# A hybrid decoder step: inputs in a second, turned layout, channel-major normalisation, token-major memory values, two outputs that leave turned

## The chip, the cores and the metric

The kernel runs on one core of a Trainium2 chip. Five engines issue their instructions in order, each from a list of its own: PE (matrix products; a transpose is a product with an identity matrix), ACT (activations, casts and copies), DVE (vector operations), POOL (GpSimd) and SP, which here only issues DMAs; ACT also issues some. An engine goes on to its next instruction only when everything that this instruction waits for is there. The metric is the device time of one execution in microseconds, as the median of several runs. The host's preparation of the arrays is not part of it.

## The reference, cut to what matters

Prompt and sample tokens (1024 and 8, 1032 together, 1024 channels each) go through one layer:

```
h    = x * rsqrt(mean(x*x) + EPS) * norm_g            # per token, over channels
proj = h @ w_in                                       # 7688 columns: q, k, v, beta, alpha, gates, ...
ya, S, buf = delta_branch(q, k, v, ...)               # causal conv, SiLU, gated delta rule
yb, vn = chunk_mlp_branch(u, v, gate, ...)            # LayerNorm, 128x128 position mixing
yc   = memory_branch(q, gate, mem_k, mem_v)           # attention into 256 memory tokens
y    = x + (sum of gates * (branch @ w_br)) @ w_out   # then a final RMSNorm

def memory_kv(mem, mem_norm_g, w_mem_kv):
    kv = rmsnorm(mem, mem_norm_g) @ w_mem_kv
    k, v = jnp.split(kv, [C_WIDTH], axis=-1)          # both are outputs: (256, 4, 128)

def causal_conv(buf, x, w):                           # 1536 channels, 4 taps
    xp = jnp.concatenate([buf.astype(x.dtype), x], axis=1)
    ...
    return jax.nn.silu(y), xp[:, -(CONV_WIDTH - 1):]  # the last three rows are an output too
```

## The kernel before, in words

**Products.** Every large product is made in three passes over a rounded high part and the rest: hi·hi, hi·lo and lo·hi, each over the KT = 8 blocks of 128 channels (`mm3`), so 24 matmuls per group. The normalised input stands channel-major, as hTh and hTl: partition = channel in its block, then block, then token. Tokens are taken in three groups of 344; one projected tile of 128 output channels (k0, v0, q0 for head 0, and so on) is 72 matmuls. `h_group` makes one group into a PSUM buffer pj, of which there are two; an `evac` function, mostly a copy on ACT, empties it. tp (two buffers) and dl (four) are the other PSUM buffers.

**Weights.** `order` lists every job's weight slice of 128 columns. `w_load` starts its load three jobs ahead, from ACT's queue; `w_split` casts it one job ahead (whi on ACT, L250) and subtracts (wlo, on DVE unless another engine is named, L253).

**Order of the work.** The order on each engine is the order in which the code emits it. The jobs run one after another as the plans say: `plan_a` (per head k, v, q, the gate ag, tiles of branch B and merge gates), `plan_c` (gates, eight kv jobs of the memory, then cq and cg) and `plan_m` (branch projections). Everything else is a generator in `Streams`: after every sixth matmul `tick` moves each generator to its next yield, so its instructions come to lie between matmuls. `run.until(condition)` moves the generators on without emitting matmuls between them.

**The start.** Rows of x are loaded token-major on SP in tiles of 128 tokens. `n_square` (L366) squares and sums on ACT, `n_newton` makes the reciprocal root in eleven small steps on DVE, `n_scale` scales rows by root and norm_g on DVE, and `n_turn` transposes eight blocks on PE, casts them to hTh on ACT (L393) and subtracts to hTl on DVE (L394). Tiles 0 and 1 are done ahead; `norm_gen` (L436) does the rest between the matmuls of k0 and v0, which run in four parts of 256, 256, 256 and 264 tokens, each as soon as its rows are ready. `const_gen` turns the small vectors and the old convolution state on PE. Then comes q0 as an ordinary job, then the product with wab, the 8 columns of beta and alpha (L583).

**The delta stream.** After that `delta_all` is added: for each head `delta_gen` (L733) waits for its k, v and q and walks through the chunks; the last chunk's products stand in L909 to L918, the result r is scaled in L931 (r by ro) and, two ticks later, turned by eight transposes, from which ag is multiplied and stored as ya. `conv_gen` (L482) runs for each k, v and q tile: it turns the last 11 columns of the raw projection (xraw, two buffers, copied in L531), copies the rows and stores them to the two state outputs, then convolves. When plan_a is through, `run.until(("delta", 3) in done)` finishes the stream.

**The memory.** `mem_norm` (L291) normalises 256 rows like the start. A kv job makes a tile of 128 columns of keys or values, channel-major (kvT, copied in L1132); `kv_gen` splits keys as they are, turns every tile on PE, stores the rows, and splits values from the rows. `b_gen` (L1034) first turns the four w_spatial blocks on PE.

The jobs of the plans and the rule of the streams, as they stand:

```python
    plan_a = [
        [("k", 0), ("v", 0), ("q", 0), ("ag", 0), ("bv", 0), ("bv", 1), ("bv", 2)],
        [("k", 1), ("v", 1), ("q", 1), ("ag", 1), ("bv", 3), ("bg", 0), ("bu", 0)] + gates(1),
        [("k", 2), ("v", 2), ("q", 2), ("ag", 2), ("bg", 1), ("bu", 1), ("bg", 2), ("bu", 2)],
        [("k", 3), ("v", 3), ("q", 3), ("ag", 3), ("bg", 3), ("bu", 3)] + gates(7),
    ]
    ...
            PE.matmul(out, lhsT=w, rhs=r, start=(i == 0), stop=(i == len(ops) - 1))
            if ticks and i % 6 == 5:
                tick()
```

Of the kernel before, what the change touches and what calls it, by code (L numbers as in the profile page):

```python
# [21 lines left out]
P = 128  # L22
# [19 lines left out]
    ("x_sample", (NB, D)),  # L42
    ("cache_mem_k", (NB, MEM, H, P)),
# [4 lines left out]
    ("norm_g", (D,)),  # L48
    ("w_in", (D, 7688)),
    ("conv_w", (4, 1536)),  # L50
    ("a_log", (H,)),
    ("dt_bias", (H,)),
    ("a_norm_g", (P,)),
    ("ln_v_g", (512,)),
    ("ln_v_b", (512,)),
    ("w_spatial", (H, P, P)),
    ("b_spatial", (H, P)),
    ("mem_norm_g", (D,)),
# [4 lines left out]
    ("b_gate", (3, D)),  # L63
# [55 lines left out]
def tile_mixer_step(ctx: ExitStack, tc: tile.TileContext, a):  # L119
# [64 lines left out]
    c_bg, c_cw, c_an = 16, 40, 88  # L184
# [8 lines left out]
    # ---- weights: loaded three jobs ahead, split one job ahead  # L193
# [7 lines left out]
    def gates(n):  # L201
# [4 lines left out]
        [("k", 0), ("v", 0), ("q", 0), ("ag", 0), ("bv", 0), ("bv", 1), ("bv", 2)],  # L206
# [83 lines left out]
    # ---- RMSNorm of the inputs, transposed and split  # L290
    def mem_norm(np_, srcs, g_bc, dst_h, dst_l):  # L291
        ss = np_.tile([P, 2], F32, tag="nss", name="mss")
        r = np_.tile([P, 2], F32, tag="nrs", name="mrs")
        xs = []
        for i, src in enumerate(srcs):
            x = np_.tile([P, D], F32, tag="x", name="x")
            SP.dma_start(out=x, in_=src)
            xs.append(x)
        yield 6
        for i, x in enumerate(xs):  # L300
            xn = np_.tile([P, D], F32, tag="xn", name="xn", bufs=2)
            S.activation(out=xn, in_=x, func=AF.Square, accum_out=ss[:, i:i + 1])
# [3 lines left out]
        for i, x in enumerate(xs):  # L306
            xn = np_.tile([P, D], F32, tag="xn", name="xn", bufs=2)
            V.scalar_tensor_tensor(
                out=xn, in0=x, scalar=r[:, i:i + 1], in1=g_bc, op0=ALU.mult, op1=ALU.mult
            )  # L310
            yield 2
            cs = slice(i * P, (i + 1) * P)
            for b in range(2):
                t = tp().rearrange("p (k n) -> p k n", k=4)
                for k in range(4):
                    kk = b * 4 + k
                    transpose(t[:, k], xn[:, kk * P:(kk + 1) * P])
                split(dst_h[:, b * 4:b * 4 + 4, cs], dst_l[:, b * 4:b * 4 + 4, cs], t)
                yield 1
            done.add(("mem", i))  # L320
# [1189 lines left out]
```

## Time and profile before

| | before |
|---|---|
| median of 3 runs | 1152.01 us |
| lowest and highest run | 1151.9 and 1152.84 us |
| span of the profiled execution | 1148.6 us |
| PE busy | 1119.7 us (97%), 7609 instructions |
| DVE busy | 609.7 us (53%) |
| ACT busy | 411.9 us (36%) |
| POOL busy | 214.1 us (19%) |
| PE's waits for scaled rows at the start | 12.7 us, 2 times, the longest 10.4 us |
| mean granted PE clock | 0.995 |

The profiled execution's own time is its span, from its first to its last instruction; the runs are timed from outside and lie 3.4 us above it in the median. A busy time is the sum over an engine's instructions; the columns "PEld" in the profile are PE's weight loads, which lie beside its products. In a row of groups stand the code line, the engine, the operation, the tile written and the tile read, shapes, the count, and then busy time and mean duration, then the idle time before them and what ended it. Line numbers are those of the kernel before; where the text says that a line is of the changed kernel, it is that one's own.

### The profile page before, as it was taken

To read this page: it belongs to the slowest core of one execution; us is meant where nothing else is said; L and a number is where in the kernel's file an instruction comes from. 1 tells how busy PE (TensorE), PEld (TensorE's weight loads), DVE (VectorE), ACT (ScalarE), POOL (GpSimd) and SP (SyncE) were. 2 spreads that over 40 slices of the span, in tenths; PEclk is the share of its full clock that TensorE was granted. 3 is DMA by queue.
4 is the path that set the end of the run, shared out by engine and by line. 5 is a ranking of instruction groups with operands and counts; after the bars stand their busy time and mean duration, and the time that the engine had idled before them with its cause. 6 is when DMAs were issued, how large, how long until landed. Compare 5 with 4: busy or idle time off the path is not lost.

```text
span 1148.6 us, 19257 instructions
## 1 busy us (share of the span) xinstructions
PE 1119.7 (97%) x7609; PEld 1074.8 (94%) x7609; DVE 609.7 (53%) x1512; ACT 411.9 (36%) x891; POOL 214.1 (19%) x392
## 2 busy tenths in 40 slices
PE   5999999999999999999999999999999999999997
PEld 4989999999999999999999999989999999998884
DVE  6754654655465546513277432655545246786554
ACT  5434233333331333333344333545445321232232
POOL 1060715070507050600034000101101000000000
PEclk9999999999999999999999999999999999999999
DMA  8104420341143114422654556543432465662221
GB/s 250 39 20 97 132 63 23 117 129 46 40 125 104 45 41 126 124 79 77 200 138 137 166 170 186 159 118 93 146 114 74 145 195 176 212 213 100 83 93 57
DMA packets 153772, 133.53 MB, mean 116 GB/s; under 512 B 20941, under 2 KB 134922, under 8 KB 153674
## 3 DMA queue, kind: packets, MB, share of 16 engines
q1 hardware_dynamic: 72242, 89.82, 24.5%
q10 hardware_dynamic: 81440, 42.49, 13.7%
q8 instruction: 60, 0.98, 0.3%
q14 instruction: 30, 0.25, 0.1%
HBM read 100.74 MB, written 31.64 MB: 115 GB/s over the span
## 4 chain that ended last, share of the span: by engine, by line
PE 90%; DVE 4%; DMA 2%; ACT 2%; issue 1%; SPq 1%; ACTq 0%; DVEq 0%
PE pj L275 56%; PE dl L275 20%; PE tp L191 2%; PE dl L191 2%; PE dl L784 1%; DMA raw<-w_in 1%; DMA stg<-ya 1%; PE dl L894 1%; PE tp L1094 1%; PE dl L918 1%; PE dl L909 1%; PE dl L902 1%; PE dl L904 1%; PE dl L917 1%; DVE wlo L253 1%
## 5 line engine op out<-in xcount | busy, mean ns | idle before, releaser
L275 PE MATMUL pj<-hTh,whi 128*128 128x344 f32 (+1 forms) x1456 | 280.7, 327 | 3.1 <-DVE ql L155 1.1
L275 PE MATMUL pj<-hTh,wlo 128*128 128x344 f32 (+1 forms) x1456 | 277.5, 325 | 0.0
L275 PE MATMUL pj<-hTl,whi 128*128 128x344 f32 (+1 forms) x1456 | 272.3, 322 | 0.0
L275 PEld LDWEIGHTS pj<-hTh,whi 128*128 128x128 f32 x1456 | 232.4, 190 | 5.9 <-ACT hTh L393 1.5
L275 PEld LDWEIGHTS pj<-hTh,wlo 128*128 128x128 f32 x1456 | 235.1, 189 | 1.4 <-issue 0.8
L275 PEld LDWEIGHTS pj<-hTl,whi 128*128 128x128 f32 x1456 | 234.3, 188 | 1.1 <-DVE hTl L394 0.2
L253 DVE TENSOR_TENSOR wlo<-raw,whi 128x1024 fp32r<-128x1024 f32 (+1 forms) x91 | 102.5, 1126 | 51.7 <-ACT whi L250 44.2
L250 ACT CAST whi<-raw 128x1024 fp32r<-128x1024 f32 (+1 forms) x92 | 86.2, 937 | 81.5 <-PE dl L275 64.8
L957 ACT COPY stg<-pj 128x344 f32<-128x344 f32 x72 | 32.1, 446 | 108.0 <-PE pj L275 107.6
L838 POOL TENSOR_TENSOR itmp<-X,Lt 128x60 f32<-128x60 f32 (+24 forms) x124 | 43.7, 352 | 125.7 <-DMA Lt<-ld 116.5
L1184 POOL TENSOR_TENSOR kvt<-kvt,qb 128x1024 f32<-128x1024 f32 x8 | 19.2, 2419 | 210.7 <-DMA qb<-qd 130.9
L275 PE MATMUL dl<-yh,whi 128*128 128x344 f32 x288 | 57.3, 321 | 0.0
L275 PE MATMUL dl<-yh,wlo 128*128 128x344 f32 x288 | 57.3, 321 | 0.0
L275 PE MATMUL dl<-yl,whi 128*128 128x344 f32 x288 | 57.1, 320 | 0.0
L275 PEld LDWEIGHTS dl<-yh,whi 128*128 128x128 f32 x288 | 47.8, 188 | 0.0
L275 PEld LDWEIGHTS dl<-yh,wlo 128*128 128x128 f32 x288 | 47.7, 188 | 0.0
L275 PEld LDWEIGHTS dl<-yl,whi 128*128 128x128 f32 x288 | 47.6, 188 | 0.0
L844 POOL TENSOR_TENSOR X<-X,itmp 128x60 f32<-128x60 f32 (+24 forms) x124 | 43.7, 353 | 9.7
L531 ACT COPY xraw<-pj 128x344 f32<-128x344 f32 (+2 forms) x38 | 16.3, 430 | 66.4 <-PE pj L275 63.1
L906 DVE COPY y<-dl 128x128 f32<-128x128 f32 x32 | 9.3, 291 | 55.3 <-PE dl L904 34.4
L1367 DVE TENSOR_TENSOR stg<-dl,stg 128x344 f32<-128x344 f32 x48 | 24.7, 515 | 18.1 <-PE dl L275 18.1
L503 POOL TENSOR_TENSOR kq<-kq,cvt 128x512 f32<-128x512 f32 x24 | 32.6, 1358 | 1.9
(378 smaller groups left out, 1591.9 us busy)
## 6 DMA issues: line engine op xcount, KB each, us to landing
raw<-w_in ACTq DMA_DIRECT2D x57, 512.0 KB
gate<-stg SPq DMA_DIRECT2D x23, 516.0 KB
stg<-gate SPq DMA_DIRECT2D x23, 516.0 KB
x<-x_prompt SPq DMA_DIRECT2D x8, 512.0 KB
raw<-w_mem_kv ACTq DMA_DIRECT2D x8, 512.0 KB
kvt<-cache_mem_k SPq DMA_DIRECT2D x16, 256.0 KB
kvt<-cache_mem_v SPq DMA_DIRECT2D x16, 256.0 KB
wor<-w_out SPq DMA_DIRECT2D x8, 512.0 KB
```

The costliest lines, as they stand in the source:

```text
L191: PE.transpose(out, in_, ident[:p, :p])
L250: S.copy(out=hi, in_=raws[i])
L253: eng.tensor_tensor(out=lo, in0=raws[i], in1=f32(hi), op=ALU.subtract)
L275: PE.matmul(out, lhsT=w, rhs=r, start=(i == 0), stop=(i == len(ops) - 1))
L503: G.tensor_tensor(out=d[:, cs], in0=d[:, cs], in1=o, op=ALU.add)
L531: S.copy(out=raw[:, 3 + sl.start:3 + sl.stop], in_=o)
L784: PE.matmul(t, lhsT=kq[:, 0, sl], rhs=kq[:, :, sl], start=True, stop=True)
L838: G.tensor_tensor(out=tm, in0=X[:, 0:m, j:j + 1].to_broadcast([P, m, n]), in1=Lt[:, j:j + 1, j + 1:32].to_broadcast([P, m, n]), op=ALU.mult,)
L844: G.tensor_tensor(out=X[:, 0:m, j + 1:32], in0=X[:, 0:m, j + 1:32], in1=tm, op=ALU.subtract)
L957: project("gate", i, lambda n, sl, o: S.copy(out=t[:, sl], in_=o))
L1184: G.tensor_tensor(out=kts[hb], in0=kts[hb], in1=qb[:, hb * 4:hb * 4 + 4].unsqueeze(2).to_broadcast([P, 4, 2, P]), op=ALU.mult,)
L1367: V.tensor_tensor(out=sg[:, sl], in0=o, in1=sg[:, sl], op=ALU.mult)
```

## The change

The host now also passes the inputs in turned layouts and turns two outputs back: `x_t` and `mem_t` are x and the memory channel-major, (128, 8, tokens); `cols` holds norm_g, mem_norm_g, b_gate, conv_w and a_norm_g as 89 columns; `conv_old` and `w_spatial_t` are the convolution state and the spatial matrices turned. `x_prompt`, `x_sample` and `mem_prompt` are still read token-major as well, for the sums of squares and the residual. The new convolution state leaves channel-major (`conv_new`, 11 columns per channel) and the memory keys leave channel-major (`mk_t`). On the device:

- 1/rms is spread over the partitions by a product of a matrix of ones with a diagonal matrix (`spread`), and x_t is scaled in place, block by block, by the channel's norm_g and that row (`scale`), then split. Transposes of x, of the memory, of the vectors, of the convolution state and of w_spatial are gone.
- The start runs over four parts of tokens; the tiles are k0, v0 and bv0, which moves ahead of q0 in plan_a.
- A convolution tile stores its 11 columns straight from xraw.
- Memory values are made token-major: four kv jobs each take two blocks of 128 input channels and all 512 value columns, adding up in two dl buffers; `v_gen` copies, splits and stores them. Memory keys are stored and split as they are made.

The core of the diff:

```diff
-        [("k", 0), ("v", 0), ("q", 0), ("ag", 0), ("bv", 0), ("bv", 1), ("bv", 2)],
+        [("k", 0), ("v", 0), ("bv", 0), ("q", 0), ("ag", 0), ("bv", 1), ("bv", 2)],
...
+    def spread(np_, rs, tiles):
+        t = dl()
+        at = 0
+        for i, n in tiles:
+            dg = np_.tile([P, P], F32, tag="dg", name="dg", bufs=2)[:n, :n]
+            V.tensor_scalar(out=dg, in0=ident[:n, :n], scalar1=rs[:n, i:i + 1], scalar2=None, op0=ALU.mult)
+            PE.matmul(t[:, at:at + n], lhsT=ones[:n], rhs=dg, start=True, stop=True)
+            at += n
+        return t[:, :at]
+
+    def scale(x, r, col, k):
+        V.scalar_tensor_tensor(
+            out=x[:, k], in0=x[:, k], scalar=colv[:, col + k:col + k + 1], in1=r, op0=ALU.mult, op1=ALU.mult
+        )
...
+    x_load(0, 1)
+    xt_load(0)
+    SP.dma_start(out=colv, in_=a["cols"])
     w_load(0, SP)
     w_load(1, SP)
+    x_load(2, 3)
+    xt_load(1)
     w_load(2, SP)
+    x_load(4)
...
+    def n_split(n, b, eng=V):
+        ks = slice(b * 4, b * 4 + 4)
+        x, hi, lo = (t[:, ks, part[n]] for t in (xT, hTh, hTl))
+        S.copy(out=hi, in_=x)
+        eng.tensor_tensor(out=lo, in0=x, in1=f32(hi), op=ALU.subtract)
+
+    def n_part(n):
+        x = xT[:, :, part[n]]
+        r = spread(np_, nrs, [(i, rows[i]) for i in in_part[n]])
+        yield
+        for b in range(2):
+            for k in range(b * 4, b * 4 + 4):
+                scale(x, r, 0, k)
+                if k % 2:
+                    yield
+            n_split(n, b, G if b else V)
+            yield
+        done.add(("norm", n))
...
     n_square(0)
     n_square(1)
-    n_square(2)
-    for _ in n_newton(0, 2, "n0"):
+    for _ in n_newton(0):
         pass
...
+    first = n_part(0)
...
+    for _ in w_split(2, slow=False, pool=np_):
+        pass
+    xt_load(2)
+    x_load(5, 6)
+    xt_load(3)
+    x_load(7, 8)
+    w_load(3)
...
     def norm_gen():
+        n_square(2)
+        n_square(3)
+        for n in range(1, 4):
+            yield
+            for i, _ in enumerate(n_newton(n)):
+                if i % 4 == 3:
+                    yield
+            yield from n_part(n)
+            if n < 3:
+                for i in in_part[n + 1]:
+                    n_square(i)
+        split(wab2[:, :, 0:8], wab2[:, :, 8:16], wab)
...
     def conv_gen(ti, dstk, raw, key):
-        t = tp()
-        transpose(t[:11, :P], raw[:, T:T + 11])
-        crow = xp.tile([11, P], F32, tag="crow", name="crow", bufs=2)
-        S.copy(out=crow, in_=t[:11, :P])
-        cs = slice(ti * P, (ti + 1) * P)
-        SP.dma_start(out=a["sc_prompt"][:, cs], in_=crow[0:3])
-        SP.dma_start(out=a["sc_sample"][:, 2, cs], in_=crow[3:11])
+        SP.dma_start(out=a["conv_new"][ti * P:(ti + 1) * P], in_=raw[:, T:T + 3 + NB])
...
+    w3 = [splits.pop(i) for i in range(3)]
     for n in range(4):
         run.until(lambda: ("norm", n) in done)
-        sl = slice(n * 256, (n + 1) * 256 if n < 3 else NT)
-        for w, ev in zip(w2, (e_k, e_v)):
-            ev(NS - 1 if n == 3 else 0, *h_group(w, n, sl))
+        for i, (w, ev) in enumerate(zip(w3, evacs)):
+            ev(NS - 1 if n == 3 else 0, *h_group(w, n, part[n]))
...
-    for kind, i in sum(plan_a, [])[3:]:
+    for kind, i in sum(plan_a, [])[4:]:
         job(kind, i)
...
+    SP.dma_start(out=wsT, in_=a["w_spatial_t"])
...
+    def kv_job(j):
+        run.until(lambda: "mem" in done)
+        w = w_next("kv", j, now=True)
         if j < H:
+            o = pj()[:, :MEM]
+            mm3(o, lambda k: w[0][:, k], lambda k: w[1][:, k], lambda k: memTh[:, k], lambda k: memTl[:, k], KT)
+            kv = mnp.tile([P, MEM], F32, tag="kvT", name="kvT")
+            S.copy(out=kv, in_=o)
+            SP.dma_start(out=a["mk_t"][j], in_=kv)
             split(kTh[:, j], kTl[:, j], kv)
+            return
+        j -= H
+        if not j:
+            v_ps.extend([dl(), dl()])
+        wh, wl = (t.rearrange("p k n -> p (k n)").rearrange("p (k n) -> p k n", k=2) for t in w)
         for m in range(2):
+            ms = slice(m * P, (m + 1) * P)
+            ops = [(l, r, k) for l, r in ((memTh, wh), (memTl, wh), (memTh, wl)) for k in range(2)]
+            for i, (l, r, k) in enumerate(ops):
+                PE.matmul(
+                    v_ps[m], lhsT=l[:, 2 * j + k, ms], rhs=r[:, k], start=(j == 0 and i == 0),
+                    stop=(j == 3 and i == len(ops) - 1),
+                )
+            tick()
+        if j == 3:
+            run.add(v_gen())
```

In the changed kernel the matmuls of `mm3` stand in L304, the spread's product in L327 (its diagonal in L326), the scale in L332, the squares in L403, the split of h in L414 and L415, the weights' cast and subtraction in L279 and L282, copies from PSUM in L533, and the transposes in L214.

More of the change, by code (lines that the diff above doesn't have):

```diff
@@ L42 @@
     ("x_sample", (NB, D)),
+    ("x_t", (P, KT, NT)),
+    ("mem_t", (P, KT, MEM)),
+    ("cols", (P, 89)),
+    ("conv_old", (P, 12, 24)),
     ("cache_mem_k", (NB, MEM, H, P)),
@@ L62 @@
     ("w_br_c", (512, D)),
-    ("b_gate", (3, D)),
     ("w_out", (D, D)),
@@ L305, in mem_norm @@
         yield from rsqrt_slow(r, ss, "m", 2)
[L306 to L320, printed above, removed]
+        t = spread(np_, r, [(0, P), (1, P)])
+        yield 1
+        for b in range(2):
+            ks = slice(b * 4, b * 4 + 4)
+            for k in range(b * 4, b * 4 + 4):
+                scale(xt, t, c_mn, k)
+                if k % 2:
+                    yield
+            split(dst_h[:, ks], dst_l[:, ks], xt[:, ks])
+            yield 1
+        done.add("mem")
     warm = const.tile([P, 1], F32, name="warm")
@@ L385, in n_turn @@
[L385 to L405 removed]
+        x = xin[i][:rows[i]]
@@ L433, in tile_mixer_step @@
+    next(first)
+    next(first)
+    wsp = [w_split(0, eng=G), w_split(1, eng=G)]
+    next(wsp[0])
+    next(first)
+    next(wsp[0], None)
+    for _ in first:
+        pass
+    next(wsp[1])
+    next(wsp[1], None)
+    for _ in w_split(2, slow=False, pool=np_):
[4 more added lines that the diff above has]
+    x_load(7, 8)
     w_load(3)
-    done.add(("norm", 0))
+    SP.dma_start(out=wab, in_=w_in_v[:, :, O_AB:O_AB + 8])
+    SP.dma_start(out=scT, in_=a["conv_old"])
+    SP.dma_start(out=a["conv_kept"], in_=a["state_conv"][:, 1:3, :])
@@ L1035, in b_gen @@
         yield 14
-        t = tp().rearrange("p (g n) -> p g n", g=H)
-        for g_ in range(H):
-            transpose(t[:, g_], wsr[:, g_])
-        S.copy(out=wsT, in_=t)
-        yield
         vn = []
@@ L1126, in kv_job, with v_gen @@
-    def kv_job(j):
-        run.until(lambda: ("mem", 1) in done)
-        w = w_next("kv", j, now=True)
-        o = pj()[:, :MEM]
-        mm3(o, lambda k: w[0][:, k], lambda k: w[1][:, k], lambda k: memTh[:, k], lambda k: memTl[:, k], KT)
-        kv = mnp.tile([P, MEM], F32, tag="kvT", name="kvT")
-        S.copy(out=kv, in_=o)
-        run.add(kv_gen(j, kv))
+    vrow = mnp.tile([P, 2, 512], F32, name="vrow", bufs=1)
+    v_ps = []
+    def v_gen():
+        for m in range(2):
+            S.copy(out=vrow[:, m], in_=v_ps[m])
+            yield
+            split(vh[:, m], vl[:, m], vrow[:, m].rearrange("p (h d) -> p h d", h=H))
+            yield
+        SP.dma_start(out=a["mv_prompt"].rearrange("(m p) c -> p m c", p=P), in_=vrow)
+        done.add("v")
```

256 lines of the change are left out of this document (92 added, 164 removed).

## The prediction

> **What bounds the kernel now.** I read the page first, then the waits of PE, then the start in order of time.
>
> ```profile
> span 1148.6 us, 19257 instructions
> PE 1119.7 (97%) x7609; PEld 1074.8 (94%) x7609; DVE 609.7 (53%) x1512; ACT 411.9 (36%) x891; POOL 214.1 (19%) x392
> PE   5999999999999999999999999999999999999997
> ...
> PE dl L191 <- DVE xn L381: 12.7, 2, 10.4
> ```
>
> PE is busy in every slice but the first and the last: what the change takes off PE's list is saved in full, and any moment in which PE waits is lost in full. The only long wait stands at the start, 12.7 us of it for the scaled rows that PE transposes. So I need three prices: PE's own work, the start, and every new place where PE waits. The start, in order of time, is this; starts, lengths, engine, line, tile, count, and in brackets the idle time before.
>
> ```profile
> 4.35 1.06 ACT L369 ACTIVATE jk<-x 128x1024 f32<-128x1024 f32 x1 [2.05 <-DMA x<-x_prompt]
> 6.54 0.19 ACT L369 ACTIVATION_READ_ACCUMULATOR jk<-x 128x1 f32 x1
> 6.76 0.17 DVE L373 TENSOR_SCALAR nss<-nss 128x2 f32<-128x2 f32 x1 [5.82 <-ACT jk L369]
> 8.73 0.16 DVE L166 SCALAR_TENSOR_TENSOR nrs<-rs_t,nrs 128x2 f32<-128x2 f32 x1
> 9.73 1.06 ACT L369 ACTIVATE jk<-x 128x1024 f32<-128x1024 f32 x1 [3.01 <-DMA x<-x_prompt]
> 15.07 1.23 PE L275 MATMUL pj<-hTh,whi 128*128 128x256 f32 x8 [1.07 <-ACT hTh L393]
> 19.45 0.63 PE L191 MATMUL dl<-ident,xn 128*128 128x128 f32 x4 [2.38 <-DVE xn L381]
> 34.60 1.11 PE L275 MATMUL pj<-hTh,whi 128*128 128x256 f32 x8
> 35.55 0.72 PE L275 MATMUL pj<-hTl,whi 128*128 128x256 f32 x4
> 60.40 1.44 PE L275 MATMUL pj<-hTh,wlo 128*128 128x344 f32 x8
> 61.68 0.32 PE L583 MATMUL pj<-hTh,wab 128*16 128x344 f32 x1
> ```
>
> Two squares with their sums take 4.35 to 6.73 (2.4 us), the eleven small DVE steps of the reciprocal root 6.76 to 8.89 (2.1). A matmul over 256 columns costs 0.95 / 8 = 0.119 us of PE. By 61.68 the tiles k0, v0 and q0 are through PE; that is the mark against which I measure the start.
>
> **The start.** On PE, tiles of 128 tokens are transposed between the matmuls of k0 and v0 (L191 before, L275 the matmuls):
>
> ```order
> L191 MATMUL dl<-ident,xn 128x128 x16
> L275 MATMUL pj<-hTh,whi 128x256 x8
> L275 MATMUL pj<-hTl,whi 128x256 x4
> L191 MATMUL dl<-ident,xn 128x128 x4
> L275 MATMUL pj<-hTl,whi 128x256 x4
> L275 MATMUL pj<-hTh,wlo 128x256 x2
> L191 MATMUL dl<-ident,xn 128x128 x4
> L275 MATMUL pj<-hTh,wlo 128x256 x6
> ```
>
> On PE in the changed kernel, same place: L304 are the matmuls of k0, v0, bv0, and L327 is the product of ones with a diagonal that spreads 1/rms over the partitions (call it the spread):
>
> ```order
> L327 MATMUL dl<-dg,ones 128x128 x2
> L304 MATMUL pj<-hTh,whi 128x256 x8
> L304 MATMUL pj<-hTl,whi 128x256 x8
> L304 MATMUL pj<-hTh,wlo 128x256 x8
> L327 MATMUL dl<-dg,ones 128x128 x2
> L304 MATMUL pj<-hTh,whi 128x256 x8
> L304 MATMUL pj<-hTl,whi 128x256 x8
> L304 MATMUL pj<-hTh,wlo 128x256 x8
> ```
>
> The 72 transposes are gone, but the second part's spread stands after only 24 matmuls; the third follows 60 matmuls later, the fourth another 60 later. Behind each, PE's matmuls queue. And on ACT, which feeds it (L403 squares, L279 weight casts, L414 casts of h, L533 copies out of PSUM):
>
> ```order
> L403 ACTIVATE x,nss<-x 128x1024 x2
> L279 CAST whi<-raw 128x1024
> L414 CAST hTh<-xT 128x4x256 x2
> L279 CAST whi<-raw 128x1024 x2
> L271 DMA raw<-w_in 128x8x128
> L403 ACTIVATE x,nss<-x 128x1024 x2
> L533 COPY xraw<-pj 128x256
> ```
>
> The squares of x2 and x3 now stand behind the cast of the third weight tile. What each step costs:
>
> ```profile
> 0.00:8.60 8.60, 0.00 (x0) 0.00 (x0) 1.60 (x11) 3.78 (x6) 0.85 (x7) 1.00 0.77 244
> 0.00:10.00 10.00, 0.00 (x0) 0.00 (x0) 2.93 (x13) 4.05 (x7) 0.85 (x7) 1.00 0.82 259
> 10.00:18.00 8.00, 5.61 (x28) 4.83 (x28) 5.82 (x17) 7.40 (x13) 2.44 (x3) 1.00 1.08 351
> 18.00:20.00 2.00, 0.55 (x5) 0.58 (x6) 1.98 (x2) 0.54 (x2) 0.00 (x0) 1.00 1.04 386
> 20.60:24.10 3.50, 3.50 (x19) 3.50 (x18) 3.19 (x9) 1.07 (x3) 0.00 (x0) 0.52 0.74 190
> ...
> L785 DVE SCALAR_TENSOR_TENSOR LA<-dl,cj,E 128x256 f32<-128x256 f32 x32 | 14.4, 483 | 9.4 <-PE dl L784 8.6 <-ACT E L773 0.8
> L253 DVE TENSOR_TENSOR wlo<-raw,whi 128x1024 fp32r<-128x1024 f32 x67 | 86.1, 1284 | 51.7 <-ACT whi L250 44.2 <-DMA wsr<-w_spatial 5.5 <-PE tp L191 1.7
> L250 ACT CAST whi<-raw 128x1024 fp32r<-128x1024 f32 x68 | 71.3, 1049 | 13.8 <-PE pj L275 12.7 <-DMA raw<-w_in 0.6
> ...
> 534.92 0.39 PE L917 MATMUL dl<-S,gcb 128*128 128x128 f32 x2
> 535.14 0.39 PE L918 MATMUL dl<-y,LA 128*128 128x128 f32 x2
> ```
>
> (The windows give busy us of PE, PEld, DVE, ACT, POOL, then PE's clock, DMA share and GB/s.) The third weight tile is the tenth load on SP: x0 to x3, two 1 MB pieces of x_t, cols and three weights make 5.8 MB. The old kernel had moved 2.6 MB by 10 us and 5.4 by 18; at 351 GB/s 5.8 MB are moved at 19.1. A load ends a little later than its bytes: x2, the fourth load, is complete with 2.1 MB, which were moved by 8.6 (244 GB/s), and it was used at 9.73. So 20.5; 18.5 if the 386 GB/s of 18 to 20 held from 10 us on, 22 if the shorter runs of x_t (1 KB, for which no row stands) are slower than 351. Then cast 1.05, two squares 2.4, root 2.1, two diagonals (no row; between the 0.16 of a tiny DVE step and the 0.48 of L785; I take 0.2 each), handovers 0.25: the second spread at 26.7. PE has by then done its 24 matmuls; the wait is about 3 us.
>
> From one spread to the next everything hangs in one chain, since each engine issues in order: two products of 0.22 (L917 to L918), four scales of 0.46 (L785, a little overlapped) 1.85, cast 1.05, DVE subtraction 1.28, four scales 1.85, cast 1.05, two squares 2.4, root 2.1, diagonals 0.4, handovers 0.7: 13.1 us. PE has 60 matmuls for it, 7.1 us. Third spread 39.8; fourth, with a third square of 1.2 and one more small diagonal, 54.3. Then 0.7 of spread and two full groups of three tiles, 72 x 0.119 and, for the last part's 264 columns, 72 x 0.123: 17.4. That makes 72.4. The loads of x and x_t for these parts (9.5 MB by 33 us at 351 GB/s) are ahead of the chain and cost nothing; without that cover each would add what it is late.
>
> The clock: after 2.38 us idle the trace grants 0.52 from 20.6 to 24.1, 1.7 us lost. The waits ahead of the third and the fourth spread are about 4 and 7 us. After the fourth the loss lies on the path (1.7), after the third mostly beside the scales (0.8): 2.5. End of the start 74.9, against 61.7: **+13.2**, bounds +6.5 (18.5 for the load, 12 per chain, no clock loss) to +17.5 (22, slow diagonals, both clock losses whole).
>
> The Trainium skill, "TensorE: Matmul & The Clock Gate", Part 1, halves the clock only after an idle window of about 3.4 us that runs free; taken strictly, the 2.4 us gap of this trace was too short, and a 4 us gap need not hold a whole window. By that rule only the fourth spread's loss is sure and the sum would be 2.5 us lower; the row of 20.6 speaks against it, and I keep the row.
>
> **The end of the delta stream.** The stream of the delta rule starts after q0 and advances one step per six matmuls of other jobs. bv0, now ahead of q0 in four parts, takes 96 matmuls (before: 72, behind q0), so the stream starts 96 matmuls later and the plan ends only 24 later. Its end loses cover. Last chunk on PE before (L918 the last product, L191 the turn of the result r, L275 projections):
>
> ```order
> L909 MATMUL dl<-y,kd 128x128
> L917 MATMUL dl<-S,gcb 128x128
> L918 MATMUL dl<-y,LA 128x128
> L275 MATMUL pj<-hTh,whi 128x344 x8
> L275 MATMUL pj<-hTl,whi 128x344 x8
> L275 MATMUL pj<-hTh,wlo 128x344 x8
> L275 MATMUL pj<-hTh,whi 128x344 x8
> L275 MATMUL pj<-hTl,whi 128x344 x4
> L191 MATMUL dl<-ident,r 128x128 x4
> ```
>
> On PE after (L926 is the last product, L214 the turn):
>
> ```order
> L917 MATMUL dl<-y,kd 128x128
> L925 MATMUL dl<-S,gcb 128x128
> L926 MATMUL dl<-y,LA 128x128
> L214 MATMUL dl<-ident,r 128x128 x8
> L304 MATMUL pj<-hTh,whi 128x344 x8
> ```
>
> The 36 covering matmuls are gone. What they covered:
>
> ```profile
> 538.16 0.39 PE L918 MATMUL dl<-y,LA 128*128 128x128 f32 x2
> 538.30 1.50 PE L275 MATMUL pj<-hTh,whi 128*128 128x344 f32 x8
> 541.77 1.23 DVE L931 TENSOR_TENSOR r<-r,ro 128x1024 f32<-128x1024 f32 x1
> 544.08 0.60 PE L191 MATMUL dl<-ident,r 128*128 128x128 f32 x4
> ...
> 559.80 1.06 ACT L302 ACTIVATE xn<-x 128x1024 f32<-128x1024 f32 x1 [4.66 <-DMA x<-mem_prompt]
> ```
>
> PE was free at 538.30, r was ready at 543.0, and 0.15 to hand over: 4.85 us of wait. One clock loss of 1.7 follows (or, in its place, ACT held up by memory rows that now load only after this point, as at 559.80): **+6.6**, bounds 4.5 to 9.
>
> **What goes from PE behind the start.**
>
> ```profile
> 63.52 0.28 PE L191 MATMUL tp<-ident,xraw 128*11 128x128 f32 x1 [0.75 <-ACT xraw L531]
> 63.56 0.40 PE L583 MATMUL pj<-hTh,wab 128*16 128x344 f32 x1
> 570.17 0.60 PE L191 MATMUL tp<-ident,xn 128*128 128x128 f32 x4
> 570.53 1.19 PE L275 MATMUL pj<-hTh,whi 128*128 128x344 f32 x6
> 702.07 1.07 PE L275 MATMUL pj<-memTl,whi 128*128 128x256 f32 x8
> 702.97 1.07 PE L275 MATMUL pj<-memTh,wlo 128*128 128x256 f32 x8
> 704.51 0.44 PE L191 MATMUL tp<-ident,kvT 128*128 128x128 f32 x2 [0.46 <-ACT kvT L1132]
> 704.70 1.50 PE L275 MATMUL pj<-hTh,whi 128*128 128x344 f32 x8
> 1061.64 1.98 PE L275 MATMUL dl<-wol,mh 128*128 128x512 f32 x8
> 1063.45 1.98 PE L275 MATMUL dl<-woh,ml 128*128 128x512 f32 x8
> ```
>
> Ten turns of the convolution's tail at 0.1 (0.04 by starts to 0.28 by their own length) and the wait of 0.75: 1.75. Four turns of memory rows at 0.36 for four, and w_spatial's four: 1.8. Eight pairs of kvT at 0.16 and the wait of 0.46: 1.75. Two spreads come in, 0.45. The value product is even: 96 matmuls at 0.90 / 8 against 48 at 1.81 / 8, 10.8 us and 10.9. Together **-4.9** (bounds -3.5 and -6.5). The rest lies beside other jobs and costs nothing while it does: mk_t, the DVE scales of the memory, bv0's copies on ACT and its store on SP, which only branch B reads much later. One wait is new: ACT's copy into xraw now waits for conv_new's DMA of the tile two before, which queues on SP behind the delta stream's transfers; behind it on ACT queue the copies that free PE's PSUM buffers. A whole tile of 72 matmuls (72 x 0.16, from 60.40 to 61.68) lies between, 11.4 us, and I book nothing.
>
> Sum: 13.2 + 6.6 - 4.9 = +14.9. The profiled execution spans 1148.6, and the runs' median 1152.0 lies 3.4 above it; with that offset kept, 1148.6 + 14.9 + 3.4 = **1166.9 us**.
>
> **The rivals.**
> 1. Faster: the chain keeps pace with 60 matmuls, that is, takes 7.1 us or less. PE would then start at about 14.3, lose some 5.4 inside the first group, and do 288 matmuls (34.6) and four spreads (2): 56.3, -5.4 instead of +13.2. With the other terms -3.7: 1148.3. For it: PE's work does shrink. Against: the rows of the chain add up to nearly twice 7.1. Chance 0.06.
> 2. The chain is shorter, about 10 us (squares and roots overlap), and the load lands early: fourth spread near 46, start +4.5; total +6: 1158. Chance 0.15.
> 3. The clock does not drop after gaps of 4 to 5 us: 2.5 less at most: 1164.4. The Trainium skill's rule above comes to this. Chance 0.12.
> 4. The memory rows land late: ACT's square stands ahead of a copy out of PSUM, and PE stalls 3 to 5 us more, with both clock losses whole: 1172. For it: 559.80 shows ACT already waiting 4.66 us there. Chance 0.15.
>
> **How the numbers follow.** The forecast has 0.50, rivals 0.06, 0.15, 0.12, 0.15, and 0.02 for a result within 0.2% (2.3 us, about what a measurement of this kernel can tell from no change). Leaving out rival 1 and the edges, the range is 1157 to 1174. Faster 0.06, same 0.02, slower 0.92.
>
> **What would show it.** In the changed profile: PE waits on DVE for dg (L326) three times in the first 60 us, the longest ahead of the fourth spread; PE's clock near 0.5 behind two of them; wab's first matmul near 86 (74.9 and q0's 11.4); one wait of nearly 5 us on DVE r around 560 to 575; fewer PE instructions after that and no wait for xraw. I would be wrong if spreads follow one another in 8 us, or if the turn of r in the last head shows no wait.

## The result and the profile after

The changed kernel takes 1172.2 us (median of 4 runs, 1170.75 to 1176.77) against 1152.42 (4 runs, 1151.9 to 1156.81); the ratio is 1.0169, 95% interval 1.0143 to 1.0196. It is slower by some 20 us; the profiled execution spans 1169.2 us, 20.6 more than before. The four runs of the changed kernel differ among themselves, and their mean granted PE clock goes with the time: 0.991, 0.988, 0.991 and 0.985 at 1170.94, 1173.47, 1170.75 and 1176.77 us. The page of the changed kernel, its first lines and PE's row of slices:

```profile
span 1169.2 us, 18948 instructions
PE 1116.4 (95%) x7474; PEld 1067.1 (91%) x7474; DVE 614.6 (53%) x1531; ACT 402.5 (34%) x854; POOL 238.2 (20%) x397
PE   3799999999999999999799999899999999999997
```

PE has 135 instructions fewer and is 3.3 us less busy, and the kernel is 20.6 longer: PE waits more. Slices 2, 20 and 26 show where. PE's waits (what was waited for; total us, times, the longest; ql is the low part of branch C's queries, ptl, further below, that of its attention weights; gp holds the delta stream's decay gates, stg is a staging tile that ACT fills from PSUM):

```profile
PE dl L327 <- DVE dg L326: 20.2, 4, 9.6
PE pj L304 <- ACT hTh L414: 6.9, 2, 4.0
PE dl L214 <- DVE r L939: 4.6, 1, 4.6
PE pj L304 <- DVE ql L178: 3.2, 1, 3.2
PE pj L304 <- ACT stg L986: 2.2, 1, 2.2
PE tp L640 <- DVE gp L636: 1.6, 1, 1.6
PE pj L304 <- ACT stg L965: 1.4, 1, 1.4
```

Cut at the same places of the program, the two executions compare so (bv0's 72 matmuls, 11.4 us at 0.159, are counted to the start in both):

| stretch | before | after | difference | forecast |
|---|---|---|---|---|
| start, to the first product with wab | 73.1 | 85.4 | +12.3 | +13.2 |
| from there to the end of plan_a | 477.6 | 483.4 | +5.8 | +4.9 |
| memory and branch C | 356.1 | 356.7 | +0.6 | -3.1 |
| branch projections | 136.7 | 136.5 | -0.2 | 0 |
| output projection to the end | 105.1 | 107.2 | +2.1 | 0 |

(Forecast: the delta stream's end +6.6 with the convolution's turns -1.75 in the second row, the rest of the turns in the third.) **The start** on PE, in order of time (start, length, count, in brackets the wait before):

```profile
27.19 1.01 PE L327 MATMUL dl<-dg,ones 128*128 128x128 f32 x4 [2.93 <-DVE dg L326]
39.72 0.71 PE L327 MATMUL dl<-dg,ones 128*128 128x128 f32 x4 [3.16 <-DVE dg L326]
53.55 1.75 PE L327 MATMUL dl<-dg,ones 128*128 128x128 f32 x6 [4.49 <-DVE dg L326]
73.93 1.42 PE L304 MATMUL pj<-hTh,whi 128*128 128x344 f32 x8
85.36 0.31 PE L591 MATMUL pj<-hTh,wab 128*16 128x344 f32 x1
```

The spreads come at 27.2, 39.7 and 53.6, that is 12.5 and 13.8 us apart. PE has 60 matmuls for each of these gaps; in part at half clock, they take 8.7 and 8.9 us (27.85 to 36.56 and 40.19 to 49.07). q0 starts at 73.9. PE's clock is halved behind each of these waits and behind that of r; windows of the changed kernel, in which the first number after the length is PE's busy time and the third from the end the granted clock:

```profile
24.04:27.45 3.41, 0.48 (x4) 0.27 (x3) 2.90 (x14) 0.37 (x1) 0.00 (x0) 1.00 1.04 377
27.45:30.86 3.41, 3.41 (x18) 3.41 (x18) 1.65 (x4) 0.93 (x1) 0.00 (x0) 0.50 1.12 337
37.69:41.10 3.41, 1.38 (x12) 1.38 (x12) 2.49 (x13) 0.00 (x0) 0.00 (x0) 1.00 0.00 0
41.10:44.51 3.41, 3.41 (x19) 3.41 (x18) 1.80 (x4) 1.32 (x2) 0.00 (x0) 0.50 0.00 0
47.93:51.34 3.41, 1.14 (x10) 0.93 (x8) 0.27 (x2) 3.32 (x7) 2.14 (x1) 1.00 0.00 0
51.34:54.75 3.41, 1.20 (x5) 0.97 (x5) 2.23 (x13) 0.00 (x0) 0.00 (x0) 0.50 0.00 0
54.75:58.17 3.42, 3.42 (x16) 3.40 (x16) 1.69 (x5) 1.07 (x1) 0.00 (x0) 0.50 0.00 0
563.34:566.75 3.41, 0.00 (x0) 0.00 (x0) 2.97 (x14) 2.27 (x3) 0.00 (x0) 1.00 0.52 144
566.75:570.16 3.41, 2.96 (x13) 2.99 (x14) 2.04 (x4) 0.00 (x0) 0.00 (x0) 0.50 0.49 186
```

**The delta stream's end, the memory rows, branch C and the output projection**, PE with the rows of DVE, ACT and SP that it hangs on:

```profile
562.23 0.39 PE L926 MATMUL dl<-y,LA 128*128 128x128 f32 x2
565.83 1.22 DVE L939 TENSOR_TENSOR r<-r,ro 128x1024 f32<-128x1024 f32 x1
567.20 1.94 PE L214 MATMUL dl<-ident,r 128*128 128x128 f32 x8 [4.58 <-DVE r L939]
...
580.97 1.06 ACT L348 ACTIVATE x<-x 128x1024 f32<-128x1024 f32 x1 [7.02 <-DMA x<-mem_prompt]
582.50 1.52 PE L304 MATMUL pj<-hTh,whi 128*128 128x344 f32 x8 [1.40 <-ACT stg L965]
...
720.55 1.42 PE L304 MATMUL pj<-hTh,whi 128*128 128x344 f32 x8
722.01 0.39 SPq L1118 DMA_DIRECT2D mv_prompt<-vrow  x1
727.16 1.67 SPq L1332 DMA_DIRECT2D stg<-ya  x2
733.33 1.05 ACT L1338 CAST yh<-stg 128x1032 fp32r<-128x1032 f32 x1 [8.33 <-DMA stg<-ya]
734.76 0.52 DVE L178 TENSOR_TENSOR ql<-pj,qh 128x344 fp32r<-128x344 f32 x1 [9.21 <-ACT qh L177]
...
1062.00 2.03 PE L304 MATMUL dl<-woh,mh 128*128 128x512 f32 x8
1063.87 2.03 PE L304 MATMUL dl<-wol,mh 128*128 128x512 f32 x8
```

The turn of r waits 4.58 us for the scaling of r, as nothing is queued between. ACT waits for the memory rows with a square that stands ahead of a copy out of PSUM, and PE loses 1.40. At branch C ACT waits for the load of ya ahead of the casts of cq, and PE loses 3.18. In the kernel before the same load and wait are these (cq's first matmul there stands at 704.70):

```profile
708.08 2.83 SPq L1319 DMA_DIRECT2D stg<-ya  x2
717.47 1.20 PE L275 MATMUL pj<-hTh,whi 128*128 128x344 f32 x6 [1.09 <-DVE ql L155]
```

In the output projection the matmuls follow one another in 1.87 / 8 = 0.233 us, where the rows of before show 1.81 / 8 = 0.227: over 384 of them 2.5 us, with no wait at all.

### The profile page after: what moved, and what is told of

Its sections match the earlier page's. It is cut to its first block, busy times and chain, and to the rows that moved or that the text cites. A ratio compares the mean times of both kernels' runs of the same rounds, so it can differ in the third digit from the quotient of the medians.

```text
span 1169.2 us, 18948 instructions
## 1 busy us (share of the span) xinstructions
PE 1116.4 (95%) x7474; PEld 1067.1 (91%) x7474; DVE 614.6 (53%) x1531; ACT 402.5 (34%) x854; POOL 238.2 (20%) x397
## 3 DMA queue, kind: packets, MB, share of 16 engines
q10 hardware_dynamic: 78368, 42.49, 13.8%
## 4 chain that ended last, share of the span: by engine, by line
PE 83%; DVE 6%; DMA 5%; ACT 3%; SPq 2%; issue 1%; ACTq 0%; POOL 0%; DVEq 0%
PE pj L304 49%; PE dl L304 20%; PE tp L214 1%; PE dl L214 1%; PE dl L792 1%; DMA raw<-w_in 1%; DVE wlo L282 1%; PE dl L1140 1%; DMA x<-mem_prompt 1%; PE dl L926 1%; PE dl L902 1%; PE tp L1092 1%; PE dl L917 1%; PE dl L910 1%; ACT x L403 1%
## 5 line engine op out<-in xcount | busy, mean ns | idle before, releaser
L304 PE MATMUL pj<-hTh,whi 128*128 128x344 f32 (+2 forms) x1464 | 283.1, 328 | 14.2 <-ACT hTh L414 6.9
L304 PE MATMUL pj<-hTh,wlo 128*128 128x344 f32 (+2 forms) x1464 | 276.8, 324 | 0.0
L304 PE MATMUL pj<-hTl,whi 128*128 128x344 f32 (+2 forms) x1464 | 271.0, 323 | 0.4 <-POOL hTl L415 0.4
L304 PEld LDWEIGHTS pj<-hTh,whi 128*128 128x128 f32 x1464 | 234.9, 192 | 17.6 <-ACT hTh L414 7.5
L304 PEld LDWEIGHTS pj<-hTl,whi 128*128 128x128 f32 x1464 | 237.0, 190 | 1.4 <-POOL hTl L415 0.7
L304 PEld LDWEIGHTS pj<-hTh,wlo 128*128 128x128 f32 x1464 | 234.9, 189 | 1.5 <-issue 0.8
L282 DVE TENSOR_TENSOR wlo<-raw,whi 128x1024 fp32r<-128x1024 f32 (+1 forms) x90 | 100.1, 1113 | 48.3 <-ACT whi L279 48.0
L279 ACT CAST whi<-raw 128x1024 fp32r<-128x1024 f32 (+1 forms) x92 | 86.1, 936 | 77.8 <-PE dl L304 68.1
L846 POOL TENSOR_TENSOR itmp<-X,Lt 128x60 f32<-128x60 f32 (+24 forms) x124 | 51.5, 415 | 170.5 <-DMA Lt<-ld 161.2
L304 PE MATMUL dl<-yh,whi 128*128 128x344 f32 x288 | 57.3, 321 | 0.0
L304 PE MATMUL dl<-yl,whi 128*128 128x344 f32 x288 | 57.1, 320 | 0.0
L304 PE MATMUL dl<-yh,wlo 128*128 128x344 f32 x288 | 57.1, 320 | 0.0
L852 POOL TENSOR_TENSOR X<-X,itmp 128x60 f32<-128x60 f32 (+24 forms) x124 | 48.4, 391 | 9.7
L304 PEld LDWEIGHTS dl<-yl,whi 128*128 128x128 f32 x288 | 47.7, 188 | 0.0
L304 PEld LDWEIGHTS dl<-yh,whi 128*128 128x128 f32 x288 | 47.7, 188 | 0.0
L304 PEld LDWEIGHTS dl<-yh,wlo 128*128 128x128 f32 x288 | 47.5, 188 | 0.0
L533 ACT COPY xraw<-pj 128x344 f32<-128x344 f32 (+2 forms) x38 | 16.3, 430 | 77.4 <-PE pj L304 77.3
```

The source lines that it names most:

```text
L279: S.copy(out=hi, in_=raws[i])
L282: eng.tensor_tensor(out=lo, in0=raws[i], in1=f32(hi), op=ALU.subtract)
L533: S.copy(out=raw[:, 3 + sl.start:3 + sl.stop], in_=o)
L846: G.tensor_tensor(out=tm, in0=X[:, 0:m, j:j + 1].to_broadcast([P, m, n]), in1=Lt[:, j:j + 1, j + 1:32].to_broadcast([P, m, n]), op=ALU.mult,)
L852: G.tensor_tensor(out=X[:, 0:m, j + 1:32], in0=X[:, 0:m, j + 1:32], in1=tm, op=ALU.subtract)
```

## The experiments

Theory A is the account of the prediction: a serial chain sets the start, bv0's new place costs the delta stream its cover, the rest of the change gains. Its rivals are named with each run. Ratios are to the kernel before on the same chip; the changed kernel has 1.0169.

**Two tiles in the start** (bv0 back behind ag0):

```diff
-        [("k", 0), ("v", 0), ("bv", 0), ("q", 0), ("ag", 0), ("bv", 1), ("bv", 2)],
+        [("k", 0), ("v", 0), ("q", 0), ("ag", 0), ("bv", 0), ("bv", 1), ("bv", 2)],
...
-        for i, (w, ev) in enumerate(zip(w3, evacs)):
+        for w, ev in zip(w2, evacs):
```

> The changed kernel, but the start works on k0 and v0 alone and bv0 is again a job behind ag0. Theory A (the start is set by the serial chain of spread, scales, splits, squares and root, 13 us per part, whatever PE has to do meanwhile; and bv0's place costs cover at the delta stream's end): the fourth spread stays near 52 to 54 us, the two tiles end near 62 to 63, bv0 costs 11.4 us later, so the start is even; the turn of r in the last head finds no wait, which gives back 4.6 us and the half clock behind it, 1.7. Time 1166. Rival C (the third tile fills PE's waits, so that its 72 early matmuls are nearly free): the start loses up to 8.6 us and the delta end gives 6.3, time 1174.

Measured: 1173.63 us, ratio 1.0193 (1.0175 to 1.0212), not to be told from the changed kernel's (1.0143 to 1.0196). PE in that run from the fourth spread on:

```profile
52.77 1.74 PE L327 MATMUL dl<-dg,ones 128*128 128x128 f32 x6 [1.70 <-DVE dg L326]
...
61.52 0.76 PE L304 MATMUL pj<-hTh,whi 128*128 128x264 f32 x4 [1.78 <-ACT hTh L414]
...
64.03 1.25 PE L304 MATMUL pj<-hTl,whi 128*128 128x264 f32 x4 [1.26 <-POOL hTl L415]
...
69.81 1.43 PE L304 MATMUL pj<-hTh,whi 128*128 128x344 f32 x8
```

The spreads stay where they were, as theory A has it, and r's wait is gone. But q0 starts at 69.8, not at 63: with fewer matmuls per part PE now also waits for the casts and subtractions behind each spread. With bv0's 11.4 us that is 81.2 against 73.9, so the third tile was worth 7.3 us, most of what rival C says. And the gain at the delta stream's end, 6.3, is eaten by branch C, where the wait on ql is 5.1 us in this run and a half clock of 6.8 us follows, 3.4 us lost, which the changed kernel's profile does not have there. (This profile is of the slowest of the run's four executions, so this last sum holds for it alone.) My forecast for this run failed in the first point.

**Squares and roots one part earlier:**

```diff
             n_split(n, b, G if b else V)
+            if not b and n < 3:
+                for i in in_part[n + 1]:
+                    n_square(i)
             yield
...
+        yield
         for n in range(1, 4):
-            yield
-            for i, _ in enumerate(n_newton(n)):
-                if i % 4 == 3:
-                    yield
-            yield from n_part(n)
-            if n < 3:
-                for i in in_part[n + 1]:
-                    n_square(i)
+            p = n_part(n)
+            yield next(p)
+            next(w2g, None)
+            yield from p
+            if n < 3:
+                for i, _ in enumerate(n_newton(n + 1)):
+                    if i % 4 == 3:
+                        yield
```

> The changed kernel, but the squares and roots of each part are made one part earlier (squares behind the first split, root behind the last scales), so that the chain between spreads is spread, scales, two splits alone, some 8 us, and x5 and x6 are loaded ahead of the third piece of x_t. Theory A: PE is then bound by its own 72 matmuls per part; no wait over 2 us for the second to fourth spread, the first matmul of q0 at 57 to 60 instead of 73.9, no half clock behind the spreads; time 1172 - 15 = 1157. Rival B (the loads of x and x_t set the pace, 9.5 MB at 350 GB/s): the waits go over to DMA and the start ends at 70 or later; time 1169 to 1172.

Measured: 1168.14 us, ratio 1.0146 (1.0128 to 1.0163), a gain of a few us at best. In order of time on POOL, DVE and PE:

```profile
33.84 0.16 DVE L188 SCALAR_TENSOR_TENSOR rs_t<-rs_t,nss 128x2 f32<-128x2 f32 x1
33.90 2.34 POOL L415 TENSOR_TENSOR hTl<-xT,hTh 128x1024 fp32r<-128x1024 f32 x1 [9.77 <-ACT hTh L414]
34.04 2.22 DVE L189 SCALAR_TENSOR_TENSOR nrs<-rs_t,nrs 128x2 f32<-128x2 f32 x1
36.29 0.16 DVE L187 TENSOR_TENSOR rs_t<-nrs 128x2 f32<-128x2 f32 x1
37.22 0.71 PE L327 MATMUL dl<-dg,ones 128*128 128x128 f32 x4 [3.67 <-DVE dg L326]
...
71.17 1.42 PE L304 MATMUL pj<-hTh,whi 128*128 128x344 f32 x8
```

Both sides were wrong here. The spreads are still 12.4 and 11.2 us apart although the loads are in by 34 us (DMA share 0.02 from 34 to 42), so rival B falls, even if its mark (q0 at 70 or later) and nearly its time came; and theory A's 8 us fall too. A DVE step over two columns, 0.16 us as a rule, takes 2.22 us and ends with POOL's subtraction, 36.26 and 36.24. The work given to POOL holds DVE back. In the changed kernel the same subtractions of the parts 1 to 3 lie in a time in which DVE waits for ACT's squares or off the chain, and cost it 0.2 us at most. But POOL's two subtractions from 18.96 to 23.69 there hold up DVE's for the third weight (L282 at 21.81 takes 2.96 us, where 1.23 is usual), so that the root of the second part begins at 24.69, 0.8 us after its squares.

The Trainium skill, "SBUF — State Buffer", section "SBUF: two separate sides", states that GpSimd and a VectorE operation with two SBUF inputs take one port pair under an exclusive lock, and the second blocks until the first is done. These rows agree with it.

**That subtraction on DVE** (on top of the early roots):

```diff
-            n_split(n, b, G if b else V)
+            n_split(n, b, G if b and not n else V)
```

> The run with early roots, but the second half's subtraction of parts 1 to 3 is made on DVE instead of POOL. Theory G (POOL's 2.4 us subtraction holds DVE's small steps for its whole length, so the work given to POOL costs DVE 2.2 us where it would take 1.2 itself, but DVE must now also wait 1.1 us for the cast ahead of it): spreads follow one another in 11 to 12 us as before, no tiny step longer than 0.3 us, time within 2 us of 1168. Rival (the long steps have another cause and POOL's help is free): DVE has 1.2 us more per part, spreads 13 us apart, time 1172.

Measured: 1171.47 us, ratio 1.016 (1.0144 to 1.0176; the run with early roots 1.0128 to 1.0163, so the two are hardly to be told apart). No small step is long any more where POOL no longer subtracts; the two of 2.25 and 2.26 us at 19.62 and 21.91, beside POOL's subtractions of the first part, stay. So the cause of the long steps is settled; but DVE now waits for a cast and subtracts itself:

```profile
34.02 1.23 DVE L415 TENSOR_TENSOR hTl<-xT,hTh 128x1024 fp32r<-128x1024 f32 x1 [1.12 <-ACT hTh L414]
35.16 0.16 DVE L408 TENSOR_SCALAR nss<-nss 128x2 f32<-128x2 f32 x1
```

That costs 2.35 us per part against 2.1 of blocking; the spreads are 12.7 and 12.0 apart, q0 starts 1.3 us later. The spreads and the time lie nearer the rival's 13 and 1172 than mine, although its reason (that POOL's help is free) is wrong.

**A start in another order** (all scales in one piece, casts and subtractions behind them, none on POOL, squares ahead, the root behind the subtractions; the third weight and x5 to x8 loaded earlier):

```diff
     def norm_gen():
+        yield 5
         for n in range(1, 4):
+            r = n_spread(n)
+            next(wsp[2], None)
+            yield 1
+            n_scale(n, r, 0)
+            yield
+            n_scale(n, r, 1)
+            yield
+            n_hi(n, 0)
+            if n < 3:
+                n_square(2 * n + 2)
+            yield 1
+            n_hi(n, 1)
+            n_lo(n, 0)
+            yield
+            n_lo(n, 1)
+            done.add(("norm", n))
...
```

> The changed kernel with a start of its own order: all eight scales of a part in one piece, both casts, both subtractions on DVE (none on POOL, whose 2.4 us subtractions hold small DVE steps of 0.16 us for 2.2 us in the run with early roots), the third weight tile loaded ahead of x_t's second piece, squares one part ahead, the root behind the subtractions. Theory A': with POOL out of it, DVE needs some 10 us per part and PE 9.5 with its spread, so PE is nearly bound by its own work: first matmul of q0 at 55 to 60, instead of 73.9 in the changed kernel and 71.2 in the run with early roots; time 1172 - 16 = 1156. Rival B (loads set the pace of the start): first matmul of q0 at 68 or later, 1166 or more.

Measured: 1158.76 us, ratio 1.0055 (1.0041 to 1.0068). PE:

```profile
41.30 1.70 PE L327 MATMUL dl<-dg,ones 128*128 128x128 f32 x6 [1.85 <-DVE dg L326]
60.48 1.42 PE L304 MATMUL pj<-hTh,whi 128*128 128x344 f32 x8
```

q0 starts 13.4 us earlier than in the changed kernel, half a microsecond later than forecast, and the time falls by 1.14%, 13 us. The same bytes are loaded, so what is loaded does not set this part of the start's loss; the order of the work does, on DVE, ACT and POOL and in the queue of loads. The edit changes all of these at once, and what each is worth was not tried apart.

**One gate job as cover of the delta stream's end:**

```diff
-        [("k", 3), ("v", 3), ("q", 3), ("ag", 3), ("bg", 3), ("bu", 3)] + gates(7),
+        [("k", 3), ("v", 3), ("q", 3), ("ag", 3), ("bg", 3), ("bu", 3)] + gates(8),
...
-        plan_c += gates(1) + [("kv", j)]
+        plan_c += gates(j < 7) + [("kv", j)]
```

> The changed kernel, but one gate job of the memory stage (the one ahead of the last kv job) runs at the end of the plan of the delta stream, so that 72 matmuls more are issued there. Theory A: the turn of r finds no wait (4.6 us) and no half clock follows (1.7): time 1166. Rival C (the wait only moves: ACT then waits longer for the memory rows, or two kv jobs in a row wait for their weights): 1170 to 1172.

Measured: 1163.02 us, ratio 1.01 (1.0083 to 1.0116), 8 us less than the changed kernel. The waits on r and for the memory rows are gone from PE's list, and of branch C's 3.2 this is left:

```profile
PE pj L304 <- DVE ql L178: 1.6, 1, 1.6
```

Wait (4.6), half clock (1.7), memory rows (1.4) and 1.6 at branch C make 9.3, less 1.7 by which its start came out later: 7.6.

**The old start with all the rest of the change:**

```diff
-    ("x_t", (P, KT, NT)),
...
+        t = dl().rearrange("p (k n) -> p k n", k=4)[:, :, :n]
+        for k in range(4):
+            kk = b * 4 + k
+            transpose(t[:, k], xns[i][:, kk * P:(kk + 1) * P])
```

> The start of before (token-major rows scaled and turned on PE, k0 and v0, bv0 behind ag0) with all the rest of the change: vectors, convolution state, convolution outputs, memory, values, w_spatial. Theory A: PE's turns behind the start are gone, 4.9 us in the sum, and the small new waits seen in the changed profile (1.4 at the memory rows, 2.1 at branch C) take back up to 3.5: time 1147 to 1151 against 1152.2. Rival D (the turned outputs and small columns cost more than the turns they replace): 1153 or more.

Measured: 1147.27 us, ratio 0.9965 (0.9952 to 0.9977): 4.1 us faster than before. So the token-major values, the turned memory, outputs, vectors and state gain together, and the new start with bv0's move costs all of the loss and more, 2.04% or 23.5 us between the two ratios. Between the profiles 2.9 us of the gain lie in the start (first product with wab at 58.80, before 61.68), and of these 1.7 are a half clock that the profile of before has behind its wait of 2.38 us and this one, behind the same wait of 2.40, has not. The run has two waits that I had not booked (before 1.1 and 0.2):

```profile
PE pj L304 <- DVE ql L178: 2.9, 1, 2.9
PE tp L655 <- DVE gp L651: 2.6, 1, 2.6
```

**The first cast of ya six ticks later** (alone, on the changed kernel):

```diff
-            yield 6
+            yield 6 if k else 12
             S.copy(out=hi, in_=raw)
```

> The changed kernel with only the first cast of the loaded ya put off by six ticks, so that it no longer stands in front of the casts of cq on ACT. Theory: the wait of 3.2 us on DVE ql at branch C vanishes and nothing takes its place, 1172 - 3 = 1169. Rival: a wait of the same size appears at the following casts, 1172.

Measured: 1167.39 us, ratio 1.0127 (1.0111 to 1.0143), 4.8 us less. The wait on ql is gone, and a later one of 1.4 us in the same stretch (on ptl) with it.

**Combinations.** The fast start with the gate as cover:

> The fast start and one gate job moved to the end of the plan of the delta stream (as in the run with cover). If the two gains stand in different places they add up: 1156 - 9 = 1147. If the stream, which now starts earlier, has its cover anyway, or the wait moves to the memory rows: 1152 to 1156.

Measured: 1148.24 us, ratio 0.9967 (0.9956 to 0.9978). The gains add up (1.14% and 0.69% off 1.0169 make 0.9986), and with the turned start the kernel has a version that beats before. It is no better than the old start with the rest of the change: PE begins q0 at 59.6 with bv0 done, the old start there at 47.4, with 11.4 us of bv0 still to come.

The same with the late cast, and gp's products two ticks later (`yield 3` to `yield 5` in `gates_gen`):

> As the run before, and two small waits of the changed profile put off: the first cast of the loaded ya, in front of the casts of cq on ACT, six ticks later (wait of 3.2 us on DVE ql), and the products of gp two ticks later (wait of 1.6 us). Theory: both waits vanish, 3 to 5 us less than the run before. Rival: other waits take their place, within 1 us of it.

Measured: 1150.24 us, ratio 0.9987 (0.9975 to 0.9999), no gain. The two waits are gone. Half clocks fall into the stretches from 134 to 139 and from 400 to 406 us (granted clock 0.66 and 0.72). The two ticks may have shifted the delta stream, but they were not tried without the late cast. Other waits now stand in that stream:

```profile
PE dl L892 <- DVE T L884: 1.8, 2, 1.0
PE dl L812 <- DVE LA L813: 1.6, 2, 1.0
PE dl L891 <- DVE TA L883: 1.2, 1, 1.2
```

The old start with the rest of the change and the same two edits:

> The old start with the rest of the change, and the same two small waits put off. Theory: waits of 2.9 on DVE ql and 2.6 on gp vanish, 1147.3 - 4 = 1143. Rival: other waits take their place, 1147.

Measured: 1142.53 us, ratio 0.9925 (0.9907 to 0.9943). This is the fastest version, 0.75% below before.

**64 bytes more in the small pool** (does the place of the merged rows make the output projection slower?):

```diff
+    sm.tile([P, 8], F32, tag="pad", name="pad")
```

> The changed kernel with one unused 64 byte place more in the small pool, which shifts later tiles by 64 bytes and changes no instruction's order. In the changed profile, and in every run with the new start, the 384 matmuls of the output projection follow one another in 233.3 ns, in before and with the old start in 226.7 ns, 2.5 us in all; the tiles of merged rows stand 64 bytes higher there, since the new start has one small tag more. Theory E (the place in the buffer decides): the step falls back to 226.7 ns and the span by 2.5 us. Rival F (the order in which PSUM's buffers take turns, which also differs and which this run keeps): 233.3 ns as in the changed kernel, no change of the time.

Measured: 1174.43 us, ratio 1.0185 (1.0171 to 1.0199), as the changed kernel. The matmuls there still follow one another in 233 ns (1068.65 less 1066.79, by 8):

```profile
1066.79 2.02 PE L304 MATMUL dl<-woh,mh 128*128 128x512 f32 x8
1068.65 2.03 PE L304 MATMUL dl<-wol,mh 128*128 128x512 f32 x8
```

A shift of 64 bytes is not the cause. The order in which PSUM's buffers take turns differs between the two groups of kernels too; that this is the cause is not shown, since it was not tried alone.

## Why the prediction was right, and where it was short

It said 1166.9 in 1157 to 1174, slower; measured 1172.2. The two mechanisms that carry the sum, the chain at the start and the lost cover at the delta stream's end, are those that the runs show. In the table the first two stretches miss by 0.9 us each, in opposite directions, and cancel; the 5 us that are missing lie in branch C and the memory (3.7) and in the output projection (2.1).

- **The start, +13.2: right.** Load of the third weight at 20.5 (its cast starts at 20.73), spreads at 26.7, 39.8 and 54.3 (27.2, 39.7, 53.6), q0 at 74.9 (73.9). The chains of 13.1 us and, with a third square, 14.5 were 12.5 and 13.8. The wait ahead of the fourth spread was 4.5 us, not 7, since PE's matmuls ran at half clock in that gap and filled more of it; where the spread stands hardly changes by that. The wab mark of 86 came at 85.4. Rivals 1 and 2, a chain of 7 or 10 us, fall. What the sum did not see is the second of the first part's casts, for which PE waits 4.0 us; it lay ahead of the second spread and cost nothing. The run with two tiles qualifies the reason: the chain sets where the spreads stand, but what PE does behind the last one depends on how many matmuls it has to fill the waits.
- **The clock, 2.5 in the start: right in kind, and on the path about right in size.** Four half windows, not two, follow the waits, 13.7 us in all. But those behind the second and the third spread mostly make PE's own matmuls longer, and PE waits again (3.16 and 4.49 us) before the next spread. Behind the fourth PE is busy for 1.20 and 3.42 us at half clock, so 2.3 us are lost on the path. By the Trainium skill, "TensorE: Matmul & The Clock Gate", Part 1, the clock is halved after an idle window of about 3.4 us; strictly taken, as rival 3 took it, PE must be idle for the whole window. At 566.75 the window before is wholly idle, and both readings agree; but the windows from 24.04, 37.69 and 47.93 hold 0.48, 1.38 and 1.14 us of products, a half clock follows each, and the waits of 2.93 and 3.16 us are shorter than a window. The measurement decides: strictly taken the rule does not hold here, and rival 3 falls. The half clock of the row of 20.6, on which the forecast rests, is itself a matter of chance: behind the same wait of 2.4 us the two profiles with the old start show none.
- **The delta stream's end, +6.6: right.** The turn waits 4.58 (4.85 said) and a half clock follows. I wrote of a clock loss "or, in its place" ACT held by memory rows; both came, the second with 1.40. Taking the cover's loss away gave 8 us, of which 1.6 lie at branch C.
- **What goes from PE behind the start, -4.9: about right in size, but the step "The rest lies beside other jobs and costs nothing while it does" failed.** The profile of the old start with the rest of the change gains 2.8 us from the product with wab to the branch projections, and it carries 4.2 us more than before in the waits on ql and gp, so the turns are worth some 7 by it; in the run with these two waits put off the gain there is 7.0, of which 2.7 are waits that before has (ql 1.1, ptl 1.4, gp 0.2) and this run has not, which leaves 4.3. The estimate is 4 to 7. By the trace it failed at the values' store, which no run moved. In the changed kernel the loads of ya start 6.6 us after the first matmul of cq (727.16 less 720.55; before 3.4, 708.08 less 704.70). On SP they stand behind the store of the token-major values, which comes at 722.01, after the last kv job, and behind the loads of the cached keys, whose first waits 1.8 us for that store. ACT's cast of ya, for which the load is awaited, stands ahead of the casts of cq: PE waits 3.2 us where before had 1.1. The late cast confirms that the wait hangs on this cast. With the memory rows' 1.4, memory and branch C came out at +0.6 instead of -3.1.
- **Not in the sum: +2.1 in the output projection**, 0.233 instead of 0.227 us per matmul, in the changed kernel and in every run with the new start; the two with the old start have 0.227. Its cause stays open.
- **Rival 4**, 1172, has the right time by luck and mostly the wrong reason: the memory rows cost 1.4, not 3 to 5; the other missing us are branch C and the output projection. The wait of ACT for conv_new's DMA, booked at nothing, did not come.

## What to carry to other kernels

Transposes that lie between matmuls of a busy TensorE may be cheap (here 0.36 us for four), and what replaces them must be priced by its waits, not by its count: here a chain across PE, DVE and ACT, in which the squares of a part stand behind the splits of the part before, set the pace. Price such a chain engine by engine against the matmuls that it must hide behind, and order the links so that the next part's are done early. When a job moves forward past the start of an interleaved stream, look at the stream's other end: it loses the cover there.

## What the runs showed of the hardware that was not expected

A half clock followed windows of 3.41 us in which PE was busy for as much as 1.38 us in the changed kernel. Counted so in all 13 profiles, in windows that begin where the clock changes, every window at full clock with at most 1.53 us of products is followed by a half clock; between 1.54 and 1.88 both are seen; from 1.92 to 3.3 none. Busy time as the profile counts it is not all: in the kernel before, PE is busy for all of 71.96 to 75.37, 2.17 us of it with 18 products of 16 by 8 elements, and a half clock follows, as in three of the runs; the same products in the changed kernel have none behind them.

The windows lie differently against the program in each execution: they begin at 24.04 in the profile of the changed kernel and at 23.11 in that of the kernel with 64 bytes more. The wait of 2.4 us at the start of before falls so that its windows hold 2.04 and 1.31 us of products, and a half clock follows; in the two profiles with the old start the same wait leaves 1.92 and 1.98, and 1.98 and 1.57, and none follows. Two kernels with the same order of instructions spent 17.1 us (the changed kernel) and 27.3 us (the one with 64 bytes more) in half windows, the end apart, so at most 8.5 and 13.7 us were lost. Differences of 2 to 3 us between single profiles mean little for that reason.

POOL's subtraction of 2.34 us stretched a DVE step of 0.16 to 2.22. And the 384 matmuls of the output projection ran 3% slower without a wait, a lower clock or another order of instructions.
